# Which memory the gate passes' operands and the mLSTM core's first tiles lie on, and k weighted without GpSimd

## The chip, the cores and the metric

The kernel runs on one core of a Trainium2 chip. The time is the device time of one execution in microseconds. Three executions of the kernel before took 2309.26, 2311.11 and 2311.87 us; the median is 2311.11. The engines are TensorE (PE in the profile, its weight loads PEld), VectorE (DVE), ScalarE (ACT), GpSimd (POOL) and SyncE (SP), whose queue issues the DMA transfers.

## The reference, cut to what matters

Two sequences, of 2048 and 256 rows of 1024 numbers, run through one windowed attention layer and one bidirectional mLSTM layer, each behind an RMSNorm, and through a final RMSNorm. All of it is fp32. The change lies in the mLSTM layer:

```
q, k, v, o, z, g = split(rms_norm(x) @ w_in)          # q, k: 512 wide, v, o, z: 1024, g: 16 gates
h = mlstm(q, k, v, gates forward) + flip(mlstm(flip(q), flip(k), flip(v), gates backward))
h = h * rsqrt(mean(h * h) + eps) * head_norm          # per head; 4 heads
x = x + (h * sigmoid(o) * silu(z)) @ w_out
```

In each direction the mLSTM goes over the sequence in chunks. A state C (128 x 258 per head) is carried from chunk to chunk; each step scales it and adds the products of k, weighted by w = exp(...) of the gates, with v. The scale factors come from a running maximum over the chunks. Inside a chunk, num = P v + sc (q C), with P = exp(D - m) * (q k^T), where D is masked to one side of the diagonal.

## The kernel before, in words

The 2304 rows are NT = 18 tiles of 128 rows. A fp32 operand is split into a high part, rounded by a cast on ScalarE (xhi, whi, kh, vh, Eh), and the rest, a subtraction on VectorE (xlo, wlo, kl, v, El); a product is three matmuls. Split weights lie in 29 slots of 4 KB: w0 to w15, y0 to y7 (pool wy, right side of the memory), x0 to x4. `slot()` gives the first one of the list `free`; what a pass has used goes back at its end of the list.

The mLSTM layer is made by these functions, one after the other in the program:

- `mlstm_qkv`: a Winograd pass (pairs of tiles; seven products of 4 operands each) for q and k, then a plain pass over the tiles for v and the gate columns.
- `gate_sums`: the gates. `u` is transposed and its maximum taken per chunk (um, L725), gathered on one partition (pr, umr), and a scan over the chunks follows in 68 small VectorE operations (L741, L744), each needing the one before it. Then spr = exp(...) (L748), pl and pl2 on TensorE, w (L754, L755), MT, sT and nT stored to `rows` in memory, em. Its tiles are those of a pool on the right side of the memory that ends with the function.
- `mlstm_gates_states`: the o pass and the z pass (b = 0 and 1), both Winograd passes over w_oz. The first two tiles of a pass, the plain pair, are made with the plain blocks b11, b12, b21, b22, the other pairs with b11, t2, b21, t3, t1, t4, b22. Each result is read by a sigmoid into a tile `e` (pool b2, three buffers) and, for z, a product. A result lies in one of two banks `pj` or two banks `c`/`d`, and the bank is free once the sigmoid, and where the value is multiplied too the product e (L852), have read it. Between the pairs the backward states are made (`weighted_k` with d = 1, `parts` for v, `state_update` with cu and C; pool b2s).
- `mlstm_core`: 18 tiles. `weights(t)` loads E, qT, kT, v, qs and makes S (L897) and E: E = rows + mask cm (L904), exp (L906), times S (L907), split (L908, L909). `core(t)` makes num (L926, L928) and hh. `update(t)` makes the forward state with k weighted on GpSimd (L795). `back(t - 1)` projects tile t - 1 with w_mo. The string ORDER interleaves the four. w_mo (16 parts, L167 and L171) is loaded ahead of the tile loop.

Tile pools share memory in time: a tile of a later pool waits for the earlier tiles on the same bytes (`reuse_waits="tile"`), not for the whole pool. The order of the instructions on each engine is set when the program is built, by a scheduler that simulates the engines and, of the instructions that are ready, takes the one that is first in the program. On the chip each engine takes its list in order.

## Time and profile before

| | |
|---|---|
| runs | 2309.26, 2311.11, 2311.87 us |
| profiled execution | 2308.62 us, span 2306.6 us, mean granted TensorE clock 0.987 |
| TensorE busy | 2216.3 us (96%) |
| VectorE, ScalarE, GpSimd busy | 1561.6 (68%), 1094.6 (47%), 468.2 us (20%) |
| o pass begins, z pass ends | about 1500, 1894.5 us |
| the core | from 1894.5 us to the end |

A row of a timeline has the start, the time in us, engine, line, operation and operands; in brackets the engine's idle time just before it and the operation that ended it. Consecutive like instructions are one row with their count (x4). A row of a table by stretches has for each engine the busy time and the instructions begun, then the granted clock as a share of full speed, the busy share of the DMA engines, and GB/s.

### The profile page before, as it was taken

To read this page: it belongs to the slowest core of one execution; us is meant where nothing else is said; L and a number is where in the kernel's file an instruction comes from. 1 tells how busy PE (TensorE), PEld (TensorE's weight loads), DVE (VectorE), ACT (ScalarE), POOL (GpSimd) and SP (SyncE) were. 2 spreads that over 40 slices of the span, in tenths; PEclk is the share of its full clock that TensorE was granted. 3 is DMA by queue.
4 is the path that set the end of the run, shared out by engine and by line. 5 is a ranking of instruction groups with operands and counts; after the bars stand their busy time and mean duration, and the time that the engine had idled before them with its cause. 6 is when DMAs were issued, how large, how long until landed. Compare 5 with 4: busy or idle time off the path is not lost.

```text
span 2306.6 us, 32951 instructions
## 1 busy us (share of the span) xinstructions
PE 2216.3 (96%) x11102; PEld 1763.1 (76%) x11102; DVE 1561.6 (68%) x3403; ACT 1094.6 (47%) x2503; POOL 468.2 (20%) x392
## 2 busy tenths in 40 slices
PE   8999999999899999999899999999999987999998
PEld 7767676767567888788788899978877876888887
DVE  7565656565877779778656422487888676777784
ACT  6454545454764335445434311346454355455453
POOL 3211121211001222232000000022232234333320
PEclk9999999999999999999999999999999997999999
DMA  7111111111226447667534622344465456665642
GB/s 266 48 39 49 38 49 39 49 38 40 92 65 196 152 159 239 219 214 237 172 123 145 222 92 92 122 157 154 164 215 174 146 188 222 216 197 196 209 157 69
DMA packets 170281, 326.41 MB, mean 142 GB/s; under 512 B 18784, under 2 KB 21632, under 8 KB 170112
## 3 DMA queue, kind: packets, MB, share of 16 engines
q1 hardware_dynamic: 169968, 324.30, 42.2%
q8 instruction: 88, 1.44, 0.3%
q14 instruction: 81, 0.66, 0.1%
q10 hardware_dynamic: 144, 0.01, 0.0%
HBM read 235.34 MB, written 88.89 MB: 141 GB/s over the span
## 4 chain that ended last, share of the span: by engine, by line
PE 75%; DVE 10%; DMA 5%; ACT 4%; issue 3%; POOL 2%; SPq 0%; DVEq 0%; POOLq 0%; ACTq 0%
PE pj L376 9%; PE pj L378 9%; PE pj L377 9%; PE pj L271 4%; PE pj L272 4%; PE pj L273 4%; PE ptp L527 3%; PE o L539 3%; PE d L271 3%; PE d L272 3%; PE c L273 3%; PE d L273 3%; PE c L272 3%; PE c L271 3%; DMA qs<-rows 2%
## 5 line engine op out<-in xcount | busy, mean ns | idle before, releaser
L376 PE MATMUL pj<-whi,xhi 128*128 128x512 f32 (+2 forms) x1152 | 433.8, 378 | 8.6 <-ACT whi L167 5.6
L122 ACT CAST xhi<-rawx 128x512 fp32r<-128x512 f32 x372 | 228.3, 618 | 439.9 <-PE pj L377 106.4
L378 PE MATMUL pj<-whi,xlo 128*128 128x512 f32 (+2 forms) x1152 | 422.8, 372 | 5.2 <-DVE xlo L123 4.4
L377 PE MATMUL pj<-wlo,xhi 128*128 128x512 f32 (+2 forms) x1152 | 426.4, 370 | 0.0
L123 DVE TENSOR_TENSOR xlo<-rawx,xhi 128x512 fp32r<-128x512 f32 x338 | 246.0, 732 | 81.3 <-ACT xhi L122 73.5
L376 PEld LDWEIGHTS pj<-whi,xhi 128*128 128x128 f32 x1152 | 218.1, 189 | 50.8 <-issue 8.8
L378 PEld LDWEIGHTS pj<-whi,xlo 128*128 128x128 f32 x1152 | 217.7, 189 | 49.5 <-DVE xlo L123 8.6
L377 PEld LDWEIGHTS pj<-wlo,xhi 128*128 128x128 f32 x1152 | 217.9, 189 | 37.0 <-issue 2.4
L514 ACT ACTIVATE Sm<-Sm,nm 128x384 f32<-128x384 f32 (+1 forms) x288 | 167.1, 582 | 94.3 <-DVE nm L508 87.9
L271 PE MATMUL pj<-whi,xhi 128*128 128x512 f32 x480 | 193.9, 404 | 7.2 <-DVE u L286 2.7
L272 PE MATMUL pj<-wlo,xhi 128*128 128x512 f32 x480 | 192.3, 401 | 2.9 <-DVE wlo L190 2.9
L273 PE MATMUL pj<-whi,xlo 128*128 128x512 f32 x480 | 191.6, 400 | 0.0
L503 DVE CUSTOM_DVE_ANT_0 Sm<-s,mask 128x384 f32<-128x384 f32 (+1 forms) x272 | 136.0, 530 | 72.8 <-PE s L501 69.9
L527 PE MATMUL ptp<-ident,Sm 128*128 128x128 f32 x800 | 135.5, 280 | 10.0 <-DVE PT L530 6.6
L527 PEld LDWEIGHTS ptp<-ident,Sm 128*128 128x128 f32 x800 | 94.6, 141 | 54.6 <-ACT Sm L514 19.2
L271 PE MATMUL d<-whi,xhi 128*128 128x512 f32 x320 | 128.0, 400 | 0.0
L273 PE MATMUL c<-whi,xlo 128*128 128x512 f32 x320 | 127.3, 398 | 0.0
L272 PE MATMUL c<-wlo,xhi 128*128 128x512 f32 x320 | 127.3, 398 | 0.0
L271 PE MATMUL c<-whi,xhi 128*128 128x512 f32 x320 | 127.2, 397 | 0.0
L272 PE MATMUL d<-wlo,xhi 128*128 128x512 f32 x320 | 126.7, 396 | 0.0
L273 PE MATMUL d<-whi,xlo 128*128 128x512 f32 x320 | 126.6, 396 | 0.0
L500 PE MATMUL s<-KH,Q 128*128 128x384 f32 (+1 forms) x288 | 106.1, 380 | 10.3 <-DVE mx L503 4.6
(243 smaller groups left out, 4670.8 us busy)
## 6 DMA issues: line engine op xcount, KB each, us to landing
rawx<-xn2T SPq DMA_DIRECT2D x144, 256.0 KB, 3.1
x<-x SPq DMA_DIRECT2D x108, 256.0 KB, 3.9
rawx<-xT SPq DMA_DIRECT2D x72, 256.0 KB, 2.9
raww<-w_oz SPq DMA_DIRECT2D x64, 256.0 KB, 5.1
raww<-w_qkvg SPq DMA_DIRECT2D x40, 256.0 KB, 3.8
v<-v SPq DMA_DIRECT2D x18, 516.0 KB, 3.7
rawx<-v SPq DMA_DIRECT2D x36, 258.0 KB, 2.8
rawx<-x SPq DMA_DIRECT2D x36, 256.0 KB, 3.0
```

The lines of the kernel that those rows point to most:

```text
L122: nc.scalar.copy(hi[:], src)
L123: (eng or nc.vector).tensor_sub(lo[:], src, hi[:].bitcast(F32))
L271: nc.tensor.matmul(o, xh, wh, start=i == 0 and not more, stop=False, skip_group_check=more)
L272: nc.tensor.matmul(o, xh, wl, start=False, stop=False, skip_group_check=more)
L273: nc.tensor.matmul(o, xl, wh, start=False, stop=i == 3, skip_group_check=more)
L376: nc.tensor.matmul(o[:, :n], xh, wh, start=kt == 0, stop=False)
L377: nc.tensor.matmul(o[:, :n], xh, wl, start=False, stop=False)
L378: nc.tensor.matmul(o[:, :n], xl, wh, start=False, stop=kt == KT - 1)
L500: nc.tensor.matmul(S[:, :nk, :], q, KH[:, g, win, :], start=True, stop=False)
L503: nc.vector.tensor_tensor_reduce(Sm[:, :nk], S[:, :nk], mask[:, t % 3, win, :], 1.0, MASKED, ALU.add, ALU.max, mx[:, c:c + 1])
L514: nc.scalar.activation(Sg[c][:, :nk], Sg[c][:, :nk], AF.Exp, bias=nm[:, c:c + 1], scale=HD ** -0.5, accum_out=rs[:, c:c + 1])
L527: nc.tensor.transpose(tp[:, c, :], Ss[g][c][:, j, :], self.ident[:])
```

## The change

Four parts:

1. `slot(op)`: in the o and z passes the operand b11 has y0 to y3 to itself, and b21 (o pass) or t2 (z pass) has y4 to y7; no other operand takes them. The v pass leaves y0 to y3 and one more slot unused. At the end of the z pass, the memory of these slots is that of the core's pool b3y.
2. Pools: in `mlstm_gates_states`, b2s is opened ahead of b2; in `mlstm_core`, b3v ahead of b3m. v, qs and El have one buffer in each of two pools instead of two in one. The mask cm has its place in the pool b3e and is loaded ahead of `mlstm_gates_states`. x lies in b3m.
3. The forward k is weighted by four scaled activations on ScalarE and four scalar_tensor_tensor operations on VectorE instead of a multiplication on GpSimd, a cast and a subtraction; its two staging buffers are taken from the eight for weights.
4. w_mo's load moves from ahead of the tile loop to position 6 of ORDER in tile 0, with the demand that it is issued after the last sigmoid of the z pass; fg is loaded behind it.

In the built program, the three e tiles now lie on bytes 144,320 to 150,464 of each partition, where gate_sums has tri, ones, lf, ab, be, uT, um, umr and most of rw (145,120 to 151,168). Before, they lay on 126,816 to 132,960, memory of `mlstm_qkv`. The lines of the program after are some 5 to 20 higher than before (L850 is L865, L748 is L757).

```diff
@@ slot, part, quarters, combinations
         self.wp = ctx.enter_context(tc.tile_pool(name="w", bufs=1))
+        self.own = {}
         self.free = deque((self.wp, f"w{i}") for i in range(16))
...
-    def slot(self):
-        pool, tag = self.free.popleft()
+    def slot(self, op=None):
+        own = self.own.get(op)
+        others = [x for tags in self.own.values() for x in tags]
+        pick = next(x for x in self.free if (x in own if own else x not in others))
+        self.free.remove(pick)
+        pool, tag = pick
...
-                    W[op][i] = self.part(self.quarter(src, c0, row, col, i), gk(i))
+                    W[op][i] = self.part(self.quarter(src, c0, row, col, i), gk(i), op)
...
-                W[op][i] = self.part(raw)
+                W[op][i] = self.part(raw, op=op)
@@ mlstm_qkv, ahead of the v pass
+            kept = self.first + [[x for x in self.free if x not in self.first][-1]]
+            self.free = deque(x for x in self.free if x not in kept)
             w = self.load_w(a["w_qkvg"][:, 1024:], [[512], [272, 256]])
             self.release()
+            self.free.extendleft(reversed(kept))
@@ weighted_k
+        if d == 0:
+            for h in range(MH):
+                wk = self.w[:, d, t, h:h + 1]
+                nc.scalar.activation(hi[:, h], k[:, h], AF.Copy, scale=wk)
+                nc.vector.scalar_tensor_tensor(lo[:, h], k[:, h], wk, hi[:, h].bitcast(F32), ALU.mult, ALU.subtract)
+            return hi, lo
         nc.gpsimd.tensor_mul(k, k, self.w[:, d, t, :].unsqueeze(2).to_broadcast([128, MH, DQK]))
@@ mlstm_gates_states
+            p = st.enter_context(tc.tile_pool(name="b2s", bufs=1, reuse_waits="tile"))
             pe = st.enter_context(tc.tile_pool(name="b2", bufs=2, reuse_waits="tile"))
-            p = st.enter_context(tc.tile_pool(name="b2s", bufs=1, reuse_waits="tile"))
...
-                    nc.scalar.activation(e, o, AF.Sigmoid)
+                    self.gated = nc.scalar.activation(e, o, AF.Sigmoid)
...
+                self.own = {"b11": self.first, "t2" if b else "b21": self.second}
@@ mlstm_core
-            py, pm, pv, p, pe = pool("b3y", side="right"), pool("b3m"), pool("b3v"), pool("b3"), self.early
+            py, pv, pm, p, pe = pool("b3y", side="right"), pool("b3v"), pool("b3m"), pool("b3"), self.early
...
-            cm = py.tile([128, 2, 128], F32, tag="cm", name="cm", bufs=1)
-            nc.sync.dma_start(cm[:], a["causal"])
+            cm = self.cm
             w = []
+            ring = self.rings["raww"]
+            self.rings["rawk"] = deque(ring.pop() for _ in range(2))
+            self.own = {}
...
-                v = self.parts(pv, self.v[t], "v", 2)
-                qs = (py if t % 2 else pv).tile([128, 2, MH, 128], F32, tag="qs", name="qs", bufs=1)
+                v = self.parts(pv if t % 2 else py, self.v[t], "v", 1)
+                qs = (pv if t % 2 else py).tile([128, 2, MH, 128], F32, tag="qs", name="qs", bufs=1)
...
-                El = p.tile([128, 2, MH, 128], F32R, tag="El", name="El", bufs=2)
+                El = (p if t % 2 else py).tile([128, 2, MH, 128], F32R, tag="El", name="El", bufs=1)
...
-                kw = self.weighted_k(py, t, 0, () if t < KX else ("raww",))
+                kw = self.weighted_k(pv, t, 0, ("rawk",))
...
-            if not WL:
-                w += self.load_w(a["w_mo"], [[512]] * 2, self.g[:, 2], PH3, PL3)
             for t in range(NT + 1):
...
-                    if t == 0 and i == WL and WL:
-                        w += self.load_w(a["w_mo"], [[512]] * 2, self.g[:, 2], PH3, PL3)
+                    if t == 0 and i == WL:
+                        with tc.issue_after(self.gated.ins):
+                            w += self.load_w(a["w_mo"], [[512]] * 2, self.g[:, 2], PH3, PL3)
+                        nc.sync.dma_start(fg[:], a["final_g"].to_broadcast([128, D]))
@@ run
+            ys = [(wy, f"y{i}") for i in range(8)]
+            self.free.extend(ys)
+            self.first, self.second = ys[:4], ys[4:]
...
                 self.early = ctx.enter_context(tc.tile_pool(name="b3e", bufs=2, reuse_waits="tile"))
+                self.cm = self.early.tile([128, 2, 128], F32, tag="cm", name="cm", bufs=1)
+                nc.sync.dma_start(self.cm[:], a["causal"])
                 self.mlstm_gates_states()
```

How it moves instructions, at three places. What stands in brackets is the queues that an instruction waits for. First ScalarE at the sigmoids of the o pass's plain pair, before (e is the sigmoid's tile, spr, scr and sT the exps of gate_sums, scr its w; rows between them are left out):

```order
L850 ACT_TABLE_LOAD
L850 ACTIVATE e<-pj 128x512 [waits PE_49]
L189 CAST whi<-raww 128x512 [waits DVE_49] x2
L850 ACTIVATE e<-pj 128x512 [waits DMAHW2_49,PE_49,Pool_49]
L850 ACTIVATE e<-c 128x512 [waits PE_49]
L850 ACTIVATE e<-c 128x512 [waits PE_49,Pool_49]
L748 ACT_TABLE_LOAD
L748 ACTIVATE spr<-spr 1x144 [waits DVE_49]
L755 ACTIVATE scr<-scr 128x144 [waits DVE_49]
L768 ACTIVATE sT<-MT,msc 72x128 [waits DVE_49] x2
```

and now, all of them in a row:

```order
L757 ACT_TABLE_LOAD
L757 ACTIVATE spr<-spr 1x144 [waits DVE_49]
L764 ACTIVATE scr<-scr 128x144 [waits DVE_49]
L777 ACTIVATE sT<-MT,msc 72x128 [waits DVE_49]
L811 CAST kh<-rawk 128x512 [waits DMAHW2_49,Pool_49]
L777 ACTIVATE sT<-MT,msc 72x128 [waits DVE_49]
L784 ACTIVATE scr<-scr 128x144 [waits DVE_49]
L823 COPY C<-cu 128x258 [waits PE_49]
L865 ACT_TABLE_LOAD
L865 ACTIVATE e<-pj 128x512 x2
L865 ACTIVATE e<-c 128x512 [waits Activation_49]
```

The four sigmoids (L850, now L865) stood ahead of the first exp of the gates (L748, now L757). Now three of them stand behind the last exp of the gates (L784), the cast kh and the copy of C, and behind a table load of their own; the fourth follows after two exps of E.

Second, TensorE where the plain pair (L322, now L327) ends and the first Winograd pair (L271 to L273, now L276 to L278) begins; before, with rows of the same kind left out:

```order
L322 MATMUL c<-whi,xlo 128x512
L271 MATMUL pj<-whi,xhi 128x512 [waits DVE_49]
L272 MATMUL pj<-wlo,xhi 128x512
L271 MATMUL pj<-whi,xhi 128x512 [waits DVE_49]
L271 MATMUL pj<-whi,xhi 128x512 [waits Activation_49]
L271 MATMUL c<-whi,xhi 128x512 [waits Activation_49]
L728 MATMUL pr<-ident,um 1x72 [waits DVE_49]
L273 MATMUL pj<-whi,xlo 128x512
L753 MATMUL pl_14942<-rw,ones 128x144 [waits DVE_49,PE_49]
L750 MATMUL pl<-spr,ones 128x144 [waits Activation_49]
```

and now:

```order
L327 MATMUL c<-whi,xlo 128x512
L914 MATMUL s<-qT,kT 128x128 [waits DMAHW7_49,DMAHW0_49]
L737 MATMUL pr<-ident,um 1x72 [waits DVE_49]
L762 MATMUL pl_14942<-rw,ones 128x144 [waits DVE_49,PE_49]
L759 MATMUL pl<-spr,ones 128x144 [waits Activation_49]
L769 MATMUL pm<-ones,rw 72x1 [waits DVE_49]
L782 MATMUL pM<-ident,MT 128x72 [waits DVE_49] x2
L821 MATMUL cu<-vh,kh 128x258 [waits DVE_49,Activation_49]
L276 MATMUL pj<-whi,xhi 128x512 [waits DVE_49]
L277 MATMUL pj<-wlo,xhi 128x512
```

The gates' small products pr, pl, pm, pM, the first S and nine cu were spread over the first Winograd pairs. Now they stand between the plain pair and the first Winograd pair, whose first row waits for VectorE.

Third, SP's queue at the beginning of the core; before, from the mask cm on:

```order
L872 DMA cm<-causal 128x256 [waits DMAHW5_49,PE_49]
L894 DMA Cb<-Cb_243 128x1032 [waits DMAHW6_49]
L890 DMA qs<-rows 128x2x512 [waits DMAHW7_49,PE_49]
L882 DMA qT<-qT_154 128x512 [waits DMAHW0_49]
L884 DMA kT<-kT_172 128x512 [waits DMAHW1_49]
L887 DMA E<-rows 128x2x512 [waits DMAHW2_49]
L894 DMA Cb<-Cb_244 128x1032 [waits DMAHW3_49,PE_49]
L942 DMA go<-go_225 128x1024 [waits DMAHW4_49]
```

and now, where four w_mo rows that only repeat, ahead of tile 1's qT (qT_154), are left out:

```order
L904 DMA E<-rows 128x2x512 [waits DMAHW2_49,DVE_49]
L899 DMA qT<-qT_155 128x512 [waits DMAHW3_49,Pool_49]
L114 DMA raww<-w_mo 128x512 [waits DMAHW4_49,DVE_49]
L873 DMA go_241<-e 128x512 [waits DMAHW5_49,Pool_49]
L114 DMA raww<-w_mo 128x512 [waits DMAHW6_49,DVE_49]
L899 DMA qT<-qT_154 128x512 [waits DMAHW3_49,PE_49]
L901 DMA kT<-kT_172 128x512 [waits DMAHW4_49]
L904 DMA E<-rows 128x2x512 [waits DMAHW5_49]
L1016 DMA fg<-final_g 128x1024 [waits DMAHW6_49]
```

cm, the first Cb and the first qs are no longer there: they are loaded earlier. Of w_mo's 16 loads, all of which were ahead of these rows, six now stand between tile 2's E (the first row) and tile 1's qT, kT and E.

More of the change, by code (lines that the diff above doesn't have):

```diff
@@ L48 @@
 AORDER2 = "ssppsspvpv"
-KX, WL = 0, 0
+WL = 6
 PH3, PL3 = (), ()
@@ L182, in release, with part @@
         self.taken = []
-    def part(self, raw, g=None):
+    def part(self, raw, g=None, op=None):
         nc = self.nc
-        hi, lo = self.slot()
+        hi, lo = self.slot(op)
         if g is None:
@@ L868, in mlstm_core @@
             TRP, TRT = self.sps, "s"
-            py, pm, pv, p, pe = pool("b3y", side="right"), pool("b3m"), pool("b3v"), pool("b3"), self.early
+            py, pv, pm, p, pe = pool("b3y", side="right"), pool("b3v"), pool("b3m"), pool("b3"), self.early
             ps = pool("b3ps", space=PSUM)
-            cm = py.tile([128, 2, 128], F32, tag="cm", name="cm", bufs=1)
-            nc.sync.dma_start(cm[:], a["causal"])
+            cm = self.cm
             w = []
+            ring = self.rings["raww"]
+            self.rings["rawk"] = deque(ring.pop() for _ in range(2))
+            self.own = {}
             fg = pm.tile([128, D], F32, tag="fg", name="fg", bufs=1)
-            nc.sync.dma_start(fg[:], a["final_g"].to_broadcast([128, D]))
             state = {0: None}
@@ L969, in back @@
                     yield
-                x = [p.tile([128, 512], F32, tag="x", name="x", bufs=3)[:] for b in range(2)]
+                x = [pm.tile([128, 512], F32, tag="x", name="x", bufs=3)[:] for b in range(2)]
                 for b in range(2):
@@ L1008, in run @@
         with tc.tile_pool(name="wy", bufs=1, side="right") as wy:
-            self.free.extend((wy, f"y{i}") for i in range(8))
+            ys = [(wy, f"y{i}") for i in range(8)]
+            self.free.extend(ys)
+            self.first, self.second = ys[:4], ys[4:]
             self.attn_core()
```

## The prediction

> **What bounds the kernel now.** I read the page's busy times first, then the row-by-row timeline of TensorE for rows that begin after an idle time, then the timelines of the engines named there.
>
> ```profile
> PE 2216.3 (96%) x11102; PEld 1763.1 (76%) x11102; DVE 1561.6 (68%) x3403; ACT 1094.6 (47%) x2503; POOL 468.2 (20%) x392
> 1516.27 0.40 PE L322 MATMUL c<-whi,xlo 128*128 128x512 f32 x1
> 1516.51 0.39 PE L271 MATMUL pj<-whi,xhi 128*128 128x512 f32 x1
> 1523.65 0.50 PE L271 MATMUL pj<-whi,xhi 128*128 128x512 f32 x1 [0.91 <-ACT whi L189]
> 1535.23 0.47 PE L271 MATMUL pj<-whi,xhi 128*128 128x512 f32 x1 [2.20 <-DVE u L286]
> 1550.88 0.48 PE L753 MATMUL pl<-rw,ones 1*128 1x144 f32 x2 [0.47 <-DVE rw L741]
> 1894.14 0.39 PE L273 MATMUL d<-whi,xlo 128*128 128x512 f32 x1
> 1902.65 0.55 PE L897 MATMUL s<-qT,kT 128*128 128x128 f32 x1 [8.12 <-DVE E L907]
> 1916.45 0.58 PE L926 MATMUL num<-vh,Eh 128*128 128x258 f32 x1 [11.75 <-ACT vh L785]
> 1929.28 0.36 PE L926 MATMUL num<-vh,Eh 128*128 128x258 f32 x1 [0.18 <-DVE r L932]
> 1944.08 1.05 PE L897 MATMUL s<-qT,kT 128*128 128x128 f32 x8
> ```
>
> TensorE is the bound: 96% of the span, some 90 us idle. So an edit pays only where it fills one of TensorE's holes, and costs wherever it opens one. Two places matter. At the front of the o pass the plain pair ends at 1516.5 and the first Winograd pair follows without a gap; three waits of 0.91, 2.20 and 0.47 us, 3.6 in all, are what TensorE loses up to 1551. At the front of the core it is the other way round: after the last matmul of the z pass (T = 1894.5) TensorE waits 8.12 and 11.75 us, tile 1's first num comes at T+34.8 and tile 2's S at T+49.6.
>
> **The front of the o pass: a wait is added.** Before, the sigmoids of the plain pair ran while the pair's other products were still being made, and the long gate scan came after them, between other work:
>
> ```profile
> 1508.31 1.28 ACT L850 ACT_TABLE_LOAD   x1
> 1509.60 0.60 ACT L850 ACTIVATE e<-pj 128x512 f32<-128x512 f32 x1
> 1511.88 0.67 DVE L852 TENSOR_TENSOR e<-e,pj 128x512 f32<-128x512 f32 x1
> 1524.91 0.41 DVE L725 TENSOR_REDUCE um<-uT 72x2 f32<-72x256 f32 x1
> 1530.48 0.69 DVE L249 TENSOR_TENSOR rawx<-rawx 128x512 f32<-128x512 f32 x1 [3.96 <-DMA rawx<-xn2T]
> 1535.61 0.36 DVE L741 TENSOR_TENSOR rw<-umr,rw 1x4 f32<-1x4 f32 x4
> 1539.96 0.22 DVE L741 TENSOR_TENSOR rw<-umr,rw 1x4 f32<-1x4 f32 x2
> 1540.14 0.23 DVE L744 TENSOR_TENSOR rw<-rw,be 1x4 f32<-1x4 f32 x2
> 1550.77 0.30 DVE L747 TENSOR_TENSOR spr<-rw 1x144 f32<-1x144 f32 x1
> ```
>
> With the two pools exchanged, the e tiles lie on ones, be, uT and rw, tiles of gate_sums that are read until the gates are finished. The sigmoids therefore stand behind the whole gate chain. The plain pair leaves its four results in both pj banks and both c/d banks; nothing reads them before those sigmoids, so TensorE, which takes its instructions in order, has no bank for the first Winograd pair. That is the new hole, from 1516.5 to the first e product.
>
> How long it is: (1) The scan can start when umr is there. In the trace um is ready at 1525.3, but the next DVE work waits 3.96 us for an activation tile, and the scan starts at 1535.6. In the changed order VectorE has the same work ahead of it, plus two v subtractions and one weight part, less two e products; the xn2T load is no longer queued behind the go store that waits for POOL. I take 1529; the bounds are 1526.5 (um plus three matmul and copy steps) and 1535.6 (as now). (2) The scan is 68 links. Pairs of links follow each other every 0.18 us, so a link is 0.09 and the scan 6.2 us when nothing stands between: it ends at 1535.3. (3) The rest of the chain has these rows:
>
> ```profile
> 1551.10 0.32 ACT L748 ACTIVATE spr<-spr 1x144 f32<-1x144 f32 x1 [1.16 <-DVE spr L747]
> 1555.20 0.28 DVE L754 TENSOR_TENSOR scr<-scr,pl 128x144 f32<-128x144 f32 x1
> 1555.52 0.32 ACT L755 ACTIVATE scr<-scr 128x144 f32<-128x144 f32 x1 [2.24 <-DVE scr L754]
> 1555.92 1.07 POOL L795 TENSOR_TENSOR rawk<-rawk,scr 128x512 f32<-128x512 f32 x1 [5.38 <-ACT scr L755]
> 1893.24 0.60 ACT L796 CAST kh<-raww 128x512 fp32r<-128x512 f32 x1
> 1927.96 0.69 DVE L797 TENSOR_TENSOR kl<-raww,kh 128x512 fp32r<-128x512 f32 x1 [0.34 <-ACT kh L796]
> 1920.52 0.35 ACT L808 COPY C<-cu 128x258 f32<-128x258 f32 x1
> ```
>
> pl2 0.5, its subtraction 0.3, w's exp 0.4, the weighting of k 1.1, kh 0.6, kl 0.7, em's exp and the three cu matmuls together 0.8, the copy of C 0.4, the table load 1.3, the sigmoid 0.6, the e product 0.7: 7.4, with hand-overs 7.7 us. TensorE starts the first Winograd pair at 1543.0, 26.5 us later than now.
>
> (4) ScalarE then stands in front of E(0): its exps wait for E's load, and behind them is the copy u<-pj that frees the first pj bank for its second use.
>
> ```profile
> 1562.91 0.32 SPq L771 DMA_DIRECT2D rows<-sT  x1
> 1564.08 0.40 SPq L887 DMA_DIRECT2D E<-rows  x1
> E<-rows SPq DMA_DIRECT2D x18, 512.0 KB, 5.1
> 1899.11 1.28 ACT L906 ACTIVATE E<-E,scr 128x128 f32<-128x128 f32 x4 [2.52 <-DVE E L904]
> 1544.42 0.58 ACT L283 COPY u<-pj 128x512 f32<-128x512 f32 x1
> ```
>
> The rows are stored at about 1540, the load is issued 1.2 us behind the last store (1541.1) and lands 5.1 later (1546.2); two mask additions 1.3, two exps 0.6, table 1.3, a sigmoid 0.6, table 1.3, six exps 1.9, a cast and the copy 1.2: 1554.4. Up to this point TensorE has 41 matmuls after the restart, 9.6 us, or 1552.6. So the 38 Winograd matmuls that the old order had finished at 1526.1 are finished at about 1554.4: 28.3 late, of which 3.5 is work taken forward (S(0), 12 cu, the gates' small matmuls). 24.8 lost; the later waits of 2.20 and 0.47 go with the old interleaving. **Sum here: +22 us**, between +17 (scan at 1526.5, E sooner) and +31 (scan at 1535.6, E 2 us later).
>
> The clock could add to it. After the 20 us of waits at the core:
>
> ```profile
> 1894.50:1905.00 10.50, 2.08 (x9) 1.78 (x8) 7.80 (x8) 7.68 (x15) 10.50 (x8) 0.73 0.99 360
> 1905.00:1920.00 15.00, 3.55 (x15) 3.29 (x15) 9.53 (x11) 9.19 (x24) 9.59 (x8) 0.51 0.92 335
> 1920.00:1945.00 25.00, 19.65 (x102) 16.64 (x102) 16.22 (x50) 14.32 (x42) 7.25 (x7) 0.86 0.50 166
> ```
>
> the granted clock (third number from the end) was 0.73, 0.51 and 0.86: 0.14 of 25 us is 3.5 us lost after work resumed. Were that so here, the 41 matmuls would end at 1556.1, 1.7 us after the copy; that stands inside the upper bound. The Trainium skill, "TensorE: Matmul & The Clock Gate", section "What's actually happening", has the clock at half after an idle window of about 3.4 us and back after about as long of sustained work, which as an estimate from the page is 1.7 us of lost work: the matmuls would end at 1554.3 and the sum would stay +22. The same page's section "HAM oscillation — how this bites in real kernels" speaks against any change that opens a gap longer than that; the trace agrees as far as the 0.51 above.
>
> **The front of the core: a wait is shortened.** The mask cm is loaded ahead of the o pass, so E(0) is finished there and S(1) needn't wait 8.12 us for it; v of tiles 0 to 2, qs(0) and Cb are loaded before T, because their tiles no longer wait for operand slots of the z pass. The first num then starts at T+2 to T+5, not at T+22. But this gain isn't kept whole: the 16 w_mo parts, which now lie under the z pass's last pair except the last, come into the hole.
>
> ```profile
> L167 ACT ACTIVATE whi<-raww,g x40: 707/722/727, 4.8 to 1894.6; 128x512 fp32r<-128x512 f32 x40
> L171 DVE SCALAR_TENSOR_TENSOR wlo<-raww,g,whi x40: 734/750/1789, 5.6 to 1895.9; 128x512 fp32r<-128x512 f32 x40
> 1894.99 1.12 SPq L887 DMA_DIRECT2D E<-rows  x1
> 1906.41 1.28 DVE L904 TENSOR_TENSOR E<-E,cm 128x512 f32<-128x512 f32 x2
> 1910.21 2.13 DVE L909 TENSOR_TENSOR El<-E,Eh 128x512 fp32r<-128x512 f32 x2
> ```
>
> That is 16 x 0.72 = 11.6 us of ScalarE and 16 x 0.75 = 12 us of VectorE. On SP's queue six w_mo loads, each waiting for a wlo to free its buffer, stand ahead of E, qT and kT of tile 1. So E(1), now issued at T+0.5, is issued at about T+10 (six wlo of 0.75 behind the first free buffer at T+4.5, and two loads of 0.5) and lands at T+15. Mask, exps, additions and split took 5.9 us (1906.4 to 1912.3); with half of the remaining ten casts between them, 4, and hand-overs num(1) is at T+25 or T+26 against T+34.8. Tile 2's S, which has tile 0's projection ahead of it, comes at T+42 against T+49.6. **-7 us**, between -12 (casts find free time) and +3: eight casts more ahead of the exps on each engine, 8 x 0.75, and the loads of w_mo late for the projection, 4.
>
> **Small terms.** Change from o to z pass: one cast pair less ahead of z's first operands, -0.7 by L167's row. Steady tiles: k without POOL costs four scaled activations (0.32 each, like the exps above, against one cast of 0.60: +0.7 of ScalarE a tile) and four short DVE operations instead of one (an estimate of +0.5). Over the span both engines have a quarter or more to spare, which covers it; uncovered, 18 tiles of 0.5 would be 9. TensorE is full there; I take +1 of 0 to +2. The v pass's last operand slot comes free one product later; its cast lies under tile 0's other blocks: 0 to 0.5, taken as 0.
>
> Sum: +22 - 7 - 0.7 + 1 = +15.3 on the profiled execution's 2308.6: 2323.9. The three runs lie at 2309.26 to 2311.87, their median 2.5 above the profiled one: **2326 us**.
>
> **Rivals.** (A) The forecast, 0.78: hole of about 25 us at the o pass, 7 back at the core; its own range is 2311 + 15 with +17/-12 and +31/+3, both ends together being unlikely: 2315 to 2338.
> (B) Nothing to tell, 0.07: the scan starts early (+17) and num(0) pulls the whole core up by 18, the 8.12 and 11.75 less 2: 2310. For it: everything but w_mo is loaded by T. Against it: SP's order, in which E(1) is behind w_mo.
> (C) Faster, 0.08: the e tiles come free when ones and be are last read by the scan, or VectorE's order matters less than I think, so TensorE loses no more than 5 us at the o pass where it lost 3.6; with -7 at the core this is 2305, with -12 2300. For it: the sigmoids need only 2.5 us themselves. Against it: ScalarE's order puts them behind em's exp and the copy of C, whatever frees the tiles.
> (D) Slower still, 0.07: the w_mo casts fill the core's first 25 us so that tile 1 is no sooner, +3, and tile 0's projection waits for the last of them, 5 more: 2311 + 22 + 8 = 2341. It decides when E(1) is issued later than T+18.
>
> **How the numbers follow.** 0.2%, 4.6 us, is about what a measurement of this kernel can tell from no change. A and D are slower; of A some 0.02 lies under 2315.7 and goes to "same" with B: faster 0.08 (C), same 0.09, slower 0.83. The range leaves out most of C and D: 2307 to 2338.
>
> **What would show it.** Right: in the changed profile TensorE's row of the first Winograd pair of the o pass begins near 1543 after waits that name the scan, spr and e; the sigmoids stand behind em's exp; the stretch 1516 to 1545 is nearly empty with a clock near 0.5; num(0) starts within 5 us of the z pass's end and S(2) near T+42. Wrong: a first Winograd pair before 1525 (step of the tiles), a scan that starts before 1526 or runs over 8 us (step 1, 2), E(1) issued before T+6 or after T+18 (core). If the hole is there and the time isn't longer, the core has given more than 20 us.

## The result and the profile after

The changed kernel is slower: 2329.53 us, the median of four runs (2328.35 to 2330.38), against 2310.19 us for the kernel before on the same chip (four runs, 2308.96 to 2311.87). The ratio is 1.0077 with a 95% interval of [1.0064, 1.0091]: +19.3 us. The forecast was 2326 us in a range of 2307 to 2338. The profiled execution took 2328.35 us with a span of 2326.6, 20.0 us more than the span before.

The page of the profile after, its span and the busy times of the engines:

```profile
span 2326.6 us, 33046 instructions
PE 2222.4 (96%) x11102; PEld 1766.9 (76%) x11102; DVE 1553.0 (67%) x3451; ACT 1099.0 (47%) x2548; POOL 435.5 (19%) x376
```

TensorE has the same 11102 matmuls and is busy 6 us more; the other 14 us of the longer span are added idle time. GpSimd is busy 33 us less and VectorE 9 us less, and the span is longer all the same.

The timeline of TensorE after, rows that begin behind an idle time (start, duration, engine, line, operation; in brackets the idle time and what ended it). First the front of the o pass, then the front of the core, whose z pass ends at T = 1912.15:

```profile
1525.88 0.64 PE L737 MATMUL pr<-ident,um 72*1 72x72 f32 x4 [8.35 <-DVE um L734]
1536.63 0.81 PE L762 MATMUL pl<-rw,ones 1*128 1x144 f32 x2 [10.12 <-DVE rw L750]
1539.60 0.38 PE L782 MATMUL pM<-ident,MT 72*128 72x72 f32 x1 [1.12 <-DVE MT L776]
1541.50 0.55 PE L821 MATMUL cu<-vh,kh 128*128 128x258 f32 x1 [0.74 <-DVE scr L783]
1545.58 0.79 PE L276 MATMUL pj<-whi,xhi 128*128 128x512 f32 x1 [1.61 <-DVE e L867]
1917.50 0.58 PE L943 MATMUL num<-vh,El 128*128 128x258 f32 x1 [2.61 <-DVE El L926]
1926.52 0.58 PE L821 MATMUL cu<-vh,kh 128*128 128x258 f32 x1 [5.20 <-ACT C L823]
1938.15 0.58 PE L821 MATMUL cu<-vh,kh 128*128 128x258 f32 x1 [3.58 <-ACT C L823]
1949.40 0.41 PE L984 MATMUL tr<-ident,hh 128*128 128x128 f32 x2 [3.33 <-DVE hh L961]
```

The first five rows are the hole of the forecast, with the waits it named: um, the scan (rw), the products of the gates, and the e product ahead of the first Winograd pair. That pair now starts at 1545.58, 29.1 us after the 1516.51 of before. In the core the two long waits, 8.12 and 11.75 us, are gone; four others have come in their place.

The same hole by stretches (busy time and instructions of PE, PEld, DVE, ACT and POOL, then the granted clock, the share of the DMA engines and GB/s):

```profile
1516.50:1545.00 28.50, 6.74 (x32) 5.14 (x30) 20.99 (x101) 10.23 (x19) 1.04 (x1) 0.57 0.42 136
```

How late the changed kernel is follows from the n-th Winograd matmul of the two gate passes, counted in both traces:

| Place on TensorE | before | after | lag |
|---|---|---|---|
| 1st Winograd matmul (o pass) | 1516.5 | 1545.6 | +29.1 |
| 50th | 1529.6 | 1559.9 | +30.2 |
| 200th | 1570.3 | 1596.2 | +25.9 |
| 650th (end of the o pass) | 1685.6 | 1709.0 | +23.4 |
| 750th (start of the z pass) | 1746.6 | 1765.1 | +18.5 |
| 1300th (end of the z pass) | 1883.9 | 1901.5 | +17.6 |
| end of the span | 2306.6 | 2326.6 | +20.0 |

So the whole loss arises in the first 50 us of the o pass. Between the passes 5 us come back, and in the core nothing: from T to the end of the span it takes 412.1 us before and 414.4 after.

The change between the passes, in the table of waits (who waited for what: us in all, times, longest). Of before:

```profile
PE pj L272 <- DVE wlo L190: 2.9, 1, 2.9
PE pj L271 <- DVE e L852: 2.4, 2, 1.3
```

and after:

```profile
PE pj L277 <- DVE wlo L195: 1.3, 1, 1.3
PE pj L276 <- DVE e L867: 1.2, 1, 1.2
```

One wait for a weight part is 1.6 us shorter and one of two waits for an e product is gone, 1.2 us: 2.8 of the 5.

### The profile page after: what moved, and what is told of

It is laid out like the page before. It is cut to its first block, busy times and chain, and to the rows that moved or that the text cites. A ratio compares the mean times of both kernels' runs of the same rounds, so it can differ in the third digit from the quotient of the medians.

```text
span 2326.6 us, 33046 instructions
## 1 busy us (share of the span) xinstructions
PE 2222.4 (96%) x11102; PEld 1766.9 (76%) x11102; DVE 1553.0 (67%) x3451; ACT 1099.0 (47%) x2548; POOL 435.5 (19%) x376
## 4 chain that ended last, share of the span: by engine, by line
PE 75%; DVE 10%; DMA 6%; ACT 5%; issue 3%; POOL 1%; SPq 0%; DVEq 0%; POOLq 0%; ACTq 0%
PE pj L381 9%; PE pj L383 9%; PE pj L382 9%; PE pj L276 5%; PE pj L278 5%; PE pj L277 5%; PE ptp L532 3%; PE o L544 3%; PE c L278 3%; PE c L276 3%; PE c L277 3%; PE d L276 3%; PE d L278 3%; PE d L277 3%; DMA qs<-rows 2%
## 5 line engine op out<-in xcount | busy, mean ns | idle before, releaser
L124 DVE TENSOR_TENSOR xlo<-rawx,xhi 128x512 fp32r<-128x512 f32 x338 | 238.5, 710 | 83.1 <-ACT xhi L123 71.9
L276 PE MATMUL pj<-whi,xhi 128*128 128x512 f32 x480 | 194.4, 405 | 5.1 <-DVE e L867 2.8
L278 PE MATMUL pj<-whi,xlo 128*128 128x512 f32 x480 | 192.0, 400 | 0.0
L532 PEld LDWEIGHTS ptp<-ident,Sm 128*128 128x128 f32 x800 | 94.0, 140 | 55.2 <-ACT Sm L519 19.9
L276 PE MATMUL d<-whi,xhi 128*128 128x512 f32 x320 | 127.6, 399 | 0.0
L276 PE MATMUL c<-whi,xhi 128*128 128x512 f32 x320 | 127.3, 398 | 0.0
L278 PE MATMUL c<-whi,xlo 128*128 128x512 f32 x320 | 127.0, 397 | 0.0
L278 PE MATMUL d<-whi,xlo 128*128 128x512 f32 x320 | 126.6, 396 | 0.0
L194 ACT CAST whi<-raww 128x512 fp32r<-128x512 f32 x144 | 85.6, 619 | 74.0 <-DVE raww L223 28.4
```

Source lines behind the costliest of these rows:

```text
L124: (eng or nc.vector).tensor_sub(lo[:], src, hi[:].bitcast(F32))
L194: nc.scalar.copy(hi[:], raw)
L276: nc.tensor.matmul(o, xh, wh, start=i == 0 and not more, stop=False, skip_group_check=more)
L278: nc.tensor.matmul(o, xl, wh, start=False, stop=i == 3, skip_group_check=more)
L532: nc.tensor.transpose(tp[:, c, :], Ss[g][c][:, j, :], self.ident[:])
```

## Experiments

Three explanations stood against each other for the o pass: the place of the three e tiles (the forecast), the exchange of the two pools in some other way (the operands of the backward states also moved), and something in the other three parts of the change. For the core there was the question what had taken the 7 us that were forecast: the w_mo parts in the hole, k weighted without GpSimd, or the order of the whole core. "Core" in the table is the time from T to TensorE's last instruction. "Regular from" is read from the order of TensorE's work: the stretch between the S of one tile and that of the next has, in the steady core, the same sequence in all these kernels (`s4 pj16 cu3 pj4 tr4 num12 cu3 num4 pj24 tr4 cu3 num16 pj3 cu3 pj1`, counts of the program's matmuls by target; in the trace S and the products with C are two rows each, so there it reads s8, num15, num5 and num20). Stretch 1 begins with tile 2's S, stretch 2 with tile 3's, and so on; the column tells from which of them on that sequence holds. All times are us; the ratio is to the kernel before on the same chip, which took 2308.4 us beside kernels 1 to 8 and 2311.3 us beside kernels 9 to 12, so medians of the two groups are compared by their ratios.

| Kernel | first Winograd pair | T | core | regular from | median | ratio, 95% |
|---|---|---|---|---|---|---|
| before | 1516.5 | 1894.5 | 403.9 | 5 | 2310.19 | 1 |
| after | 1545.6 | 1912.2 | 407.0 | 3 | 2329.53 | 1.0077 [1.0064, 1.0091] |
| 1: after, pools back | 1516.3 | 1892.9 | 419.1 | 9 | 2320.81 | 1.0061 [1.0038, 1.0084] |
| 2: before, pools exchanged | 1541.5 | 1908.1 | 402.7 | 4 | 2321.89 | 1.0056 [1.0035, 1.0076] |
| 3: after, w_mo early | 1544.3 | 1912.1 | 404.8 | 5 | 2327.89 | 1.0086 [1.0061, 1.0110] |
| 4: after, k on GpSimd | 1546.4 | 1913.1 | 402.9 | 3 | 2325.29 | 1.0075 [1.0054, 1.0096] |
| 5: 1 and 3 | 1517.4 | 1891.6 | 407.2 | 4 | 2310.63 | 1.0007 [0.9997, 1.0016] |
| 6: 1, 3 and 4 | 1516.3 | 1890.3 | 403.4 | 4 | 2302.21 | 0.9971 [0.9959, 0.9982] |
| 7: after, slots unbound | 1545.3 | 1912.2 | 428.3 | 8 | 2346.34 | 1.0158 [1.0143, 1.0174] |
| 8: 3 and 4 | 1546.3 | 1914.9 | 396.5 | 6 | 2321.16 | 1.0053 [1.0039, 1.0067] |
| 9: after, e tiles apart | 1516.7 | 1897.7 | 405.8 | 4 | 2311.45 | 0.9995 [0.9985, 1.0005] |
| 10: 9 and 4 | 1518.2 | 1898.1 | 407.0 | 5 | 2313.72 | 1.0015 [1.0004, 1.0025] |
| 11: 9, 3 and 4 | 1516.9 | 1895.9 | 401.0 | 4 | 2309.09 | 0.9987 [0.9976, 0.9999] |
| 12: 9 and 3 | 1517.6 | 1898.1 | 418.5 | 9 | 2324.47 | 1.0057 [1.0036, 1.0079] |

The places (first pair, T, core) are those of one profiled execution. Single executions of one kernel lie several us apart (kernel 5: 2306.3 to 2313.8 in eleven), so differences of a few us between two rows of these columns are not worked with unless they return.

### The exchange of the pools, undone and alone

Kernel 1 is the changed kernel with the two pools in their old order; kernel 2 is the kernel before with the exchange and nothing else.

```diff
# kernel 1, in mlstm_gates_states of the changed kernel
-            p = st.enter_context(tc.tile_pool(name="b2s", bufs=1, reuse_waits="tile"))
             pe = st.enter_context(tc.tile_pool(name="b2", bufs=2, reuse_waits="tile"))
+            p = st.enter_context(tc.tile_pool(name="b2s", bufs=1, reuse_waits="tile"))
# kernel 2, the same place of the kernel before: the reverse
+            p = st.enter_context(tc.tile_pool(name="b2s", bufs=1, reuse_waits="tile"))
             pe = st.enter_context(tc.tile_pool(name="b2", bufs=2, reuse_waits="tile"))
-            p = st.enter_context(tc.tile_pool(name="b2s", bufs=1, reuse_waits="tile"))
```

> The changed kernel with the two pools of mlstm_gates_states in the old order (b2 ahead of b2s), so that the e tiles lie below the gate tiles again. Theory (the e tiles wait for the gate tiles): the hole at the front of the o pass goes, TensorE waits there under 6 us in all, and the time is 2303 to 2310 us. Rival (the hole comes from the queues: cm, v and E(0) loaded earlier, or from the bound slots): the hole stays and the time is 2327 to 2331 us.

> The kernel before with one edit, b2s opened ahead of b2. Theory: the hole of the changed kernel is there, 23 us, and the time is 2328 to 2337 us. Rival (the exchange is harmless without the other parts): 2308 to 2313 us.

Kernel 1, TensorE's timeline, the first Winograd pair and the longest wait behind it:

```profile
1516.29 0.48 PE L276 MATMUL pj<-whi,xhi 128*128 128x512 f32 x1
...
1525.61 0.50 PE L276 MATMUL pj<-whi,xhi 128*128 128x512 f32 x1 [3.24 <-ACT whi L194]
```

and its ScalarE:

```profile
1512.19 0.60 ACT L865 ACTIVATE e<-pj 128x512 f32<-128x512 f32 x1
```

Kernel 2, TensorE's timeline, two rows of the hole:

```profile
1532.54 0.81 PE L753 MATMUL pl<-rw,ones 1*128 1x144 f32 x2 [8.79 <-DVE rw L741]
1541.48 0.79 PE L271 MATMUL pj<-whi,xhi 128*128 128x512 f32 x1 [1.62 <-DVE e L852]
```

The exchange makes the hole in either kernel and its undoing removes it: 29.3 us earlier in kernel 1, where the first sigmoid is back at 1512, and 25.0 later in kernel 2. Both times missed their forecast. Kernel 2 takes +0.56% with the old core (402.7 us): 2321.89 us, under the 2328 to 2337 of the theory; of the 25.0 us of the hole 13.6 are left at T. Kernel 1 brought a surprise: T was 19 us earlier than after, and its core 12 us longer, so the time stayed at +0.61%, 2320.81 us where the theory had 2303 to 2310.

### The e tiles alone moved back

Is it the e tiles, or the operands of the backward states that moved with them? Kernel 9 gives e, and behind it vh and C, pools of their own between b2s and b2, so that e ends at byte 142,208, below the 145,120 where the gates' tiles begin. vh, C and s then lie over gate tiles, so if such operands were what held TensorE, the hole would stay.

```diff
             p = st.enter_context(tc.tile_pool(name="b2s", bufs=1, reuse_waits="tile"))
+            pg = st.enter_context(tc.tile_pool(name="b2e", bufs=3, reuse_waits="tile"))
+            pt = st.enter_context(tc.tile_pool(name="b2t", bufs=1, reuse_waits="tile"))
             pe = st.enter_context(tc.tile_pool(name="b2", bufs=2, reuse_waits="tile"))
...
-                    e = pe.tile([128, 512], F32, tag="e", name="e", bufs=3)[:]
+                    e = pg.tile([128, 512], F32, tag="e", name="e", bufs=3)[:]
# vh of parts() and C: pt.tile(...) in place of p.tile(...)
```

> The changed kernel with one edit: the e tiles get a pool of their own between kl, kh, v and vh, C of pool b2s, so that they end at byte 142,208, below the first gate tile (145,120); vh and C now lie over gate tiles, s behind them. Theory (what costs is that the sigmoids' tiles wait for the gates): the first Winograd pair of the o pass starts at 1515 to 1520 us instead of 1545.6, the z pass ends at 1892 to 1896, the core (regular order from the fourth tile) takes 402 to 408 us, the time is 2299 to 2307 us. Rival (the backward operands over the gate tiles hold TensorE in the same way, since cu stands in its queue): the hole stays, 2322 us or more.

Kernel 9, TensorE's timeline:

```profile
1516.71 0.48 PE L276 MATMUL pj<-whi,xhi 128*128 128x512 f32 x1
...
1551.31 0.38 PE L782 MATMUL pM<-ident,MT 72*128 72x72 f32 x1 [1.34 <-DVE MT L776]
1553.66 0.80 PE L821 MATMUL cu<-vh,kh 128*128 128x258 f32 x2 [1.19 <-ACT vh L794]
```

2311.45 us, ratio 0.9995 [0.9985, 1.0005], against 1.0077: the place of three tiles is the whole loss. The time forecast, 2299 to 2307 us, was missed, and T was 2 us later than its range: the z pass ends some 5 us later than in kernel 1, 2.5 of them in the last two waits, on MT and on vh. And it says something about the rest of the change: with the hole gone, the other parts together are worth nothing that can be measured here.

### w_mo in the core's hole

Kernel 3 puts the load of w_mo back ahead of the tile loop; kernel 5 does so with the pools in their old order.

```diff
+            w += self.load_w(a["w_mo"], [[512]] * 2, self.g[:, 2], PH3, PL3)
             for t in range(NT + 1):
...
-                        with tc.issue_after(self.gated.ins):
-                            w += self.load_w(a["w_mo"], [[512]] * 2, self.g[:, 2], PH3, PL3)
```

> The changed kernel with w_mo loaded ahead of the tile loop as before, without the demand on the last sigmoid. Theory W (the w_mo parts in the hole ate the gain at the core's front, forecast 7 us, measured under 1): tile 2's S comes 5 us or more sooner after the z pass's end than T+46.8, and the time is 2321 to 2325 us. Rival (the gain is lost to the chain of hh and to the tiles after it, whatever w_mo does): 2328 to 2332 us.

> The changed kernel with the two pools of mlstm_gates_states in the old order and w_mo loaded ahead of the tile loop. With the pools alone put back, TensorE's order in the core is the same from tile to tile only from the ninth tile on (from the third in the changed kernel, from the fifth before), and the core took 12 us longer than in the changed kernel; here it is so from the fourth. Theory (the core's loss in that run came from the irregular order, not from the pools' places): no hole at the o pass, the z pass ends at 1892 to 1895 us, the core takes 402 to 406 us, and the time is 2296 to 2302 us. Rival (with the pools in the old order the core's first tiles wait for their memory, and it is longer whatever the order): the core takes 412 us or more and the time is 2307 us or more.

In kernel 3 tile 2's S came at T+42.3 (after: T+46.8) and tile 0's projection ended at T+58.0 (T+64.6): w_mo in the hole does cost the front of the core 4.5 to 6.6 us. But the core as a whole is only 2.2 us shorter, and the ratio, 1.0086 [1.0061, 1.0110], cannot be told from 1.0077; the time, 2327.89 us, missed the forecast of 2321 to 2325. The gain was given back late and at one place: at tile 15's S the lead is still 5.4 us, at tile 16's it is 1.9. That stretch has another order of matmuls there, takes 23.4 us in place of 19.9, and holds one long wait. Kernel 3, TensorE:

```profile
2247.23 0.50 PE L383 MATMUL pj<-whi,xlo 128*128 128x512 f32 x1 [2.95 <-DVE xlo L124]
```

Kernel 5 missed its forecast: 2310.63 us, 1.0007 [0.9997, 1.0016]. Of kernel 1's long core 12 us went, but the core took 407.2 us. Its front is ahead of the kernel before (tile 4's S at T+87.1 against T+90.3); the same stretch, from tile 15's S to tile 16's, takes 23.4 us against 18.6.

### k weighted on GpSimd again

One line in `weighted_k`, in four surroundings: on the changed kernel (4), on 5 (6), on 3 (8) and on 9 (10).

```diff
-        if d == 0:
+        if False:
             for h in range(MH):
                 wk = self.w[:, d, t, h:h + 1]
```

> The changed kernel with the forward k weighted on GpSimd, cast and subtracted as before. Theory K (the eight short operations on ScalarE and VectorE are what the steady tiles lost, 2.8 us): 2326 to 2327.5 us, with shorter waits for xlo. Rival (without them GpSimd holds up VectorE more than they cost): 2330 to 2334 us.

> As the run with the pools back and w_mo early, and the forward k weighted on GpSimd as before. Theory K (the short operations cost the core 3 to 4 us, as the core's 402.9 us against 407.0 with k on GpSimd says): 2293 to 2299 us, 3 to 4 less than without this edit. Rival (the order alone made that difference): the same time within 1.5 us or longer.

> The changed kernel with w_mo ahead of the tile loop and the forward k on GpSimd, the pools as in the change. Theory: the hole at the o pass stays (first Winograd pair at 1543 to 1547), the core gains what the two edits gain apart, 2 and 4 us: 2320 to 2325 us. Rival (they gain the same idle time twice): 2325 to 2329 us.

> The same, with the forward k weighted on GpSimd as before. Theory K: the core is 3 to 4 us shorter than without this edit, 2295 to 2304 us. Rival (the order decides, not the short operations): within 1.5 us of the run without it, or longer.

The core became shorter by 4.1 (after to 4), 3.8 (5 to 6) and 8.3 us (3 to 8), and longer by 1.2 us with the e tiles apart (9 to 10, whose ratio is 1.0015 [1.0004, 1.0025] against 0.9995). That k without GpSimd costs the core some 4 us was the theory for kernel 10, and there it failed. Of the four times, kernel 8's alone lay in the range of its theory (2321.16 us); kernel 4's ratio cannot be told from that of after, and kernel 6 gained more than forecast on kernel 5 (8.4 us, 3 to 4 forecast) but ended at 2302.21, above 2293 to 2299.

The places of S tell where the edit acts (one execution of each kernel; us that the edit adds):

| Stretch of the core | after to 4 | 5 to 6 | 3 to 8 | 9 to 10 |
|---|---|---|---|---|
| T to tile 4's S | -1.0 | +4.4 | +1.8 | +3.8 |
| tile 4's S to tile 15's | -2.7 | -3.9 | -5.7 | -2.2 |
| tile 15's S to tile 16's | -0.4 | -4.7 | -4.7 | -0.4 |

In the steady tiles GpSimd's help is worth 2 to 6 us in every pair, kernel 10 included. What differs is the order at the two ends: kernels 3 and 5 have the slow stretch of 23.4 us behind tile 15 and 8 and 6 have not, and in kernels 6, 8 and 10 the front takes longer. Why the edit changes the order at these places was not found.

Kernel 6 beats both kernels: 2302.21 us, 0.9971 [0.9959, 0.9982] of the time before. It keeps of the change the slots bound to operands, the early mask and the core's new pools and buffers (k's two staging buffers among them), and has the pool order, the w_mo load and the k weighting on GpSimd of before. Its page:

```profile
span 2301.5 us, 32973 instructions
PE 2218.7 (96%) x11102; PEld 1764.2 (77%) x11102; DVE 1563.5 (68%) x3403; ACT 1093.7 (48%) x2503; POOL 470.8 (20%) x392
```

and the longest wait of its core, in TensorE's timeline, 22 us behind T = 1890.3:

```profile
1912.21 0.58 PE L821 MATMUL cu<-vh,kh 128*128 128x258 f32 x1 [6.15 <-ACT kh L811]
```

Its T is 4.2 us earlier than before and its core 0.5 us shorter: the gain lies in the gate passes, not where the core's tiles were moved. At the 650th Winograd matmul it is level with before (1685.8 against 1685.6) and at the 750th 3.5 us ahead (1743.1 against 1746.6), so most of it is the shorter change between the passes. TensorE is busy 2.4 us more than before in a span 5.1 us shorter.

### The slots unbound

Kernel 7 takes the binding of slots to operands out of the changed kernel.

```diff
-                self.own = {"b11": self.first, "t2" if b else "b21": self.second}
```

> The changed kernel without the binding of slots to operands in the o and z passes; the hole at the o pass stays. Its order in the core is regular from the eighth tile on. Theory (the order sets the core's length): the core takes 410 to 420 us, the time is 2333 to 2343 us. Rival (the binding matters for when the slots come free): the change from o to z pass loses the 5 us that the changed kernel gained there, the core is as in the changed kernel, 405 to 409 us, and the time is 2333 to 2336 us, with the z pass's end 4 us or more later than 1912. Both may be: then 2338 and more.

The time from the 650th to the 750th Winograd matmul is 61.0 us before, 56.1 after, and 56.4 in kernel 7: the binding is not needed for the shorter change between the passes. It is 56.2 in kernel 2, where only the pools are exchanged, and 56.8 to 57.8 in kernels 1, 5, 6 and 9, where the e tiles are not on the gates' bytes. Two different edits each bring most of the 5 us; the cause stays open. Without the binding it is the core that takes longer: 428.3 us, 8 more than the forecast's upper end, and the kernel 2346.34, 1.0158. The next section says by which stretches.

### The order of the core

Kernel 1's core was long and its steady sequence came late, from the 9th stretch on. The forecasts of kernels 5 and 7 were made from the order: regular from the 4th and a core of 402 to 406 us for 5 (it took 407.2), from the 8th and 410 to 420 for 7 (428.3). Kernel 12, with the e tiles apart and w_mo early, was built with a sequence that is regular only from the 9th, and kernel 11, the same with k on GpSimd, from the 4th. If the late order decides, 12 has a long core and 11 has not, although each of 12's edits had been harmless elsewhere.

```diff
# kernel 12: kernel 9 and
+            w += self.load_w(a["w_mo"], [[512]] * 2, self.g[:, 2], PH3, PL3)
             for t in range(NT + 1):
...
-                        with tc.issue_after(self.gated.ins):
-                            w += self.load_w(a["w_mo"], [[512]] * 2, self.g[:, 2], PH3, PL3)
# kernel 11: kernel 12 and
-        if d == 0:
+        if False:
```

> e apart and w_mo early, k as in the change. In this kernel TensorE's order in the core is the same from tile to tile only from the ninth tile on. Theory (a late regular order lengthens the core, as in the two runs where it came at the eighth and ninth tile: 428 and 419 us against 396 to 407 in the others): core 412 to 430 us, time 2308 to 2326 us. Rival (the order's regularity is a bystander): core 400 to 407 us, time 2296 to 2304 us.

> The same, with w_mo loaded ahead of the tile loop too. Theory: the core as in the run with these two edits and the hole (396.5 us) or up to 6 longer, z pass's end at 1890 to 1895: 2289 to 2299 us, faster than the kernel before by 0.4% or more. Rival (w_mo's casts under the last z pair take from the o and z passes what they give the core): 2300 to 2306 us.

Kernel 12's core took 418.5 us and its time was 2324.47, both as forecast from the order. Kernel 11's core took 401.0 us, inside its range too, but its time, 2309.09 us, missed the forecast of 2289 to 2299 and is hardly under that of before (0.9987 [0.9976, 0.9999]). The busy times over 160 us of the core, beginning 80 us behind T in each, say what the long cores lack. Before:

```profile
1974.50:2134.50 160.00, 155.40 (x860) 133.62 (x859) 117.94 (x295) 83.44 (x236) 57.27 (x50) 1.00 0.60 197
```

after:

```profile
1992.20:2152.20 160.00, 155.33 (x859) 132.98 (x858) 122.05 (x319) 86.62 (x257) 50.20 (x44) 1.00 0.61 204
```

kernel 1:

```profile
1972.90:2132.90 160.00, 146.52 (x787) 124.58 (x787) 116.06 (x297) 79.90 (x227) 47.09 (x41) 0.97 0.58 191
```

kernel 7:

```profile
1992.20:2152.20 160.00, 143.52 (x768) 121.64 (x767) 107.52 (x287) 79.01 (x230) 46.05 (x41) 0.97 0.54 178
```

kernel 12:

```profile
1978.10:2138.10 160.00, 147.13 (x789) 124.56 (x789) 115.45 (x295) 79.67 (x226) 46.08 (x41) 0.97 0.58 191
```

TensorE issues 768 to 789 matmuls there instead of 860 and idles 13 to 16 us instead of 5, half of it or more in waits for xlo (4.6 to 6.5 us) and hh (2.0 to 4.1). The longest, kernel 7:

```profile
2115.55 0.80 PE L383 MATMUL pj<-whi,xlo 128*128 128x512 f32 x1 [5.65 <-DVE xlo L124]
```

Of the fourteen kernels of the table the three that settle late have cores of 418.5 to 428.3 us and the eleven others of 396.5 to 407.2. But lateness is not what costs. Kernel 8 settles at the 6th stretch and has the shortest core; its stretches 1 to 5 take 20.3 to 22.2 us, no more than steady ones (20.7 to 22.5 in kernels 3 and 8). What the three share is one and the same order: the five stretches just ahead of the steady sequence (4 to 8 in kernels 1 and 12, 3 to 7 in kernel 7) are alike matmul by matmul, by the names of what each writes and reads, and none of the eleven others has any of them. What it costs:

| | the five shared stretches | the five steady ones behind them | difference |
|---|---|---|---|
| kernel 1 | 122.8 | 107.5 | 15.3 |
| kernel 12 | 123.4 | 107.1 | 16.3 |
| kernel 7 | 126.4 | 108.6 | 17.8 |

In each kernel 11 to 14 us of the five are idle time; one of the five also has 13 matmuls more than a steady stretch, work that other orders do elsewhere. From tile 2's S to the end kernels 1 and 12 have the same order of matmuls throughout, and cores of 419.1 and 418.5 us, although the e tiles, vh, C and the w_mo load differ between them. So kernel 12 repeats kernel 1's order more than it tests a rule about late ones. That the order sets the core's length is strongly supported and not proven: no run changed it with all else held.

## Why the prediction was right, step by step

The likeliest case, A, came true: 2329.5 against 2326, inside both ranges. The hole at the o pass, which is the bulk of it, was right in mechanism and size; the total owes something to luck, as the last terms show. By its steps:

**The tiles: right, and shown.** The sigmoids stood behind the gate chain because e lay on the gates' bytes. Kernels 1 and 2 remove and make the hole with the pools, kernel 9 removes it while vh, C and s stay on the gates' bytes.

**Steps 1 and 2, the scan: right.** VectorE after (the first row of the scan, the row behind its last, and MT):

```profile
1530.43 0.36 DVE L750 TENSOR_TENSOR rw<-umr,rw 1x4 f32<-1x4 f32 x4
1536.52 0.29 DVE L756 TENSOR_TENSOR spr<-rw 1x144 f32<-1x144 f32 x1
1538.71 1.21 DVE L776 TENSOR_TENSOR_SCAN MT<-uT,msc 72x128 f32<-72x128 f32 x2
```

The scan ran from 1530.4 to 1536.5 where 1529 to 1535.3 was forecast; its length, 6.1 us, was 6.2 in the sum.

**Step 3, the rest of the chain: mis-sized, 7.7 forecast, 9.1 measured.** From the row of spr to the copy of C the sum had 4.4 us, and it took 6.0. Behind the copy of C all is as costed. ScalarE after:

```profile
1539.89 0.60 ACT L811 CAST kh<-rawk 128x512 fp32r<-128x512 f32 x1
1541.39 0.32 ACT L784 ACTIVATE scr<-scr 128x144 f32<-128x144 f32 x1 [0.60 <-DVE scr L783]
1542.52 0.37 ACT L823 COPY C<-cu 128x258 f32<-128x258 f32 x1 [0.81 <-PE cu L821]
1542.91 1.28 ACT L865 ACT_TABLE_LOAD   x1
1544.21 1.08 ACT L865 ACTIVATE e<-pj 128x512 f32<-128x512 f32 x2
...
1554.31 0.57 ACT L288 COPY u<-pj 128x512 f32<-128x512 f32 x1
```

The missing part is MT: two scans, 1.21 us together, one product on TensorE for each and their subtractions, which stand ahead of em's exp and of the cu matmuls. I had followed w to k and cu and left MT and em's preparation out. With the scan 1.2 later this makes the restart 1545.6 in place of 1543.0.

**Step 4, the copy u<-pj: right in its time, wrong as the wait.** It ran from 1554.3 to 1554.9 (forecast: ready at 1554.4), but TensorE did not wait for it: behind the restart at 1545.58 its timeline shows no idle time of 0.1 us before 1600. The forecast had the 38 Winograd matmuls 28.3 us late because of this copy; the 38th began at 1557.1 against 1526.3, 30.8 late, because of the restart and the clock. By the end of the o pass 7.4 us of this had come back, where the sum had 6.2 (the work taken forward and the two waits of before). So the lag was +23.4 and **+22** was forecast: close, by a path that differs in its last step.

**The clock: between the two prices.** TensorE after, stretches of 2 us behind the restart, columns as above:

```profile
1545.60:1547.60 2.00, 2.00 (x5) 1.61 (x6) 1.35 (x2) 1.51 (x4) 1.85 (x2) 0.50 0.19 61
1547.60:1549.60 2.00, 2.00 (x7) 1.52 (x6) 1.00 (x2) 1.97 (x4) 0.00 (x0) 0.50 0.35 131
1549.60:1551.60 2.00, 2.00 (x7) 1.59 (x6) 0.00 (x0) 1.97 (x3) 0.81 (x1) 0.66 0.00 0
1551.60:1553.60 2.00, 2.00 (x12) 1.68 (x11) 0.69 (x1) 1.99 (x7) 0.48 (x1) 1.00 0.34 127
```

At 0.50 for 4 us and 0.66 for 2, some 2.7 us of work are lost: less than the 3.5 of the rows before, more than the 1.7 that the prediction worked out from the Trainium skill, "TensorE: Matmul & The Clock Gate", section "What's actually happening"; its recovery of about 3.4 us was 4 to 6 here. In the prediction most or all of this loss vanished in the wait for the copy; as there was no such wait, it adds to the lag.

**The front of the core: the mechanism half right, the size wrong, -7 forecast, -0.4 measured** (tile 0's projection ended at T+64.6 against T+65.0, tile 3's S came at T+69.5 against T+69.9). The first num came at T+1.1 (forecast T+2 to T+5) and tile 1's num at T+26.8 (T+25 or T+26). The step that failed is the next one, tile 2's S at T+42; it came at T+46.8. Queue and ScalarE after, the issues of tile 2's E and of tile 1's, E(1), and the exps of each:

```profile
1918.08 0.37 SPq L904 DMA_DIRECT2D E<-rows  x1
1925.42 0.37 SPq L904 DMA_DIRECT2D E<-rows  x1
```

```profile
1922.95 1.28 ACT L923 ACT_TABLE_LOAD   x1 [5.08 <-DMA E<-rows]
1934.43 2.44 ACT L923 ACTIVATE E<-E,scr 128x128 f32<-128x128 f32 x8 [1.94 <-DVE E L921]
```

E(1) was issued at T+13.3, not T+10, behind the w_mo loads as forecast but later. Tile 2's E was issued ahead of it, at T+5.9, and its exps, with a table load, stand at the head of ScalarE's list, although they are needed only at T+48. They wait 5.08 us for that load, and behind them waits a copy of C that TensorE needs (5.20 us in the rows above). The exps of E(1) hold back another copy of C in the same way (3.58 us). The sum had counted what the lateness of E(1) does to num, and neither tile 2's exps nor what is queued behind exps on their engine. As tile 1's num was still only 1 to 2 us late, the rest arose behind it. From tile 1's num to tile 2's S, before and after:

```profile
1929.28:1944.08 14.80, 11.75 (x60) 9.96 (x61) 10.74 (x32) 6.56 (x18) 4.78 (x5) 0.88 0.57 188
1938.96:1958.97 20.01, 14.53 (x58) 12.07 (x58) 15.27 (x33) 10.02 (x30) 6.73 (x5) 0.72 0.47 167
```

Nearly the same matmuls take 2.8 us more at a granted clock of 0.72 in place of 0.88, and 2.4 us more are idle. So tile 2's S was 2.8 us ahead of before, not 7, and the next stretch lost most of that: 22.7 us against 20.4, with a wait of 2.07 for xlo. VectorE after, at 1947:

```profile
1947.78 4.29 DVE L961 SCALAR_TENSOR_TENSOR hh<-hh,ss,go 128x256 f32<-128x256 f32 x3
1952.65 0.47 DVE L961 SCALAR_TENSOR_TENSOR hh<-hh,ss,go 128x256 f32<-128x256 f32 x1
```

and GpSimd beside it:

```profile
1946.04 2.93 POOL L928 TENSOR_TENSOR qs<-qT,qs 128x512 f32<-128x512 f32 x2
1948.93 2.85 POOL L921 TENSOR_TENSOR E<-E,cm 128x512 f32<-128x512 f32 x2
```

Three of tile 0's hh products took 1.43 us each, as long as one GpSimd operation, and the fourth 0.47 when GpSimd was done. That is part of the fourth new wait, 3.33 us; the same transposes waited 2.31 us before. The Trainium skill, "SBUF — State Buffer", section "SBUF: two separate sides", has a VectorE operation with two SBUF inputs and a GpSimd operation that reads SBUF exclude one another for the whole instruction; the rows agree.

**The small terms.** Between the passes -0.7 was forecast by one cast pair; -5 was measured, by a cause that stays open. The rest of the core: +1 was forecast for k without GpSimd in the steady tiles, because the engines had time to spare; the four pairs of the table above give 2 to 6 us there, so that term was too small. From tile 3's S to the end of the span +2.7 was measured in all.

The forecast sum was +15.3 and the profiled difference +20.0. The two misses, 6.6 too much from the core and 4.3 too little from the change between the passes, mostly cancelled. That is luck: the total was better than its terms.

**The rivals.** C (the e tiles come free early) and B (the core gains 18) are out: first pair at 1545.6, core unchanged. D was not far off in the core, whose gain was nil, but E(1) came before T+18 and tile 0's projection was not late.

## What to carry to other kernels

Where tiles share memory in time, a new layout is a list of new waits: ask of each moved tile who is the last reader of the bytes it now lies on, and what stands behind the instruction that must wait; here three tiles on the bytes of a chain's operands cost 18 us, and moving them off gave it back (in the kernel before, the exchange alone cost 13). Where a program sets the order, an edit of a line or two can change a loop of 400 us by 12 to 21, so compare the order of the matmuls stretch by stretch before the edit is judged by its own cost. Take a change with several parts apart: this one as a whole lost 0.8%, and a part of it gained 0.3%.

## What was not expected of the hardware

The clock came back to full speed only 4 to 6 us after the restart, with matmuls issued without a gap from 1545.6 on; the stretches above show 0.50, 0.50, 0.66 and 1.00. The slow hh products are the other point: of 72 such VectorE operations, 0.48 us in the median, five took 1.48 to 1.50; the first three of these ran while GpSimd worked on qs and E of later tiles. Before, one of the 72 took 1.25.
